# Token-major projections and six gates as seven block products per pair of units, with the last modulation rows made in the merge and the output projection

## The chip, the cores and the metric

The kernel runs on one core of a Trainium2 chip. The metric is device time in microseconds for one execution of the whole layer. Besides the time there is a profile of one execution, with every instruction of each engine: PE (matrix products; PEld are its weight loads), DVE, ACT and POOL (elementwise), and SP, which here issues the DMA transfers.

## The reference

One layer of a backbone over 1024 tokens of width 1024, with 256 context tokens, in float32. What the change touches:

```python
m_lat = (silu(c) @ w_mod + b_mod).reshape(B_, 1, N_MOD, D)     # six modulation rows
h = rms_norm(x, norm_mix) * (1.0 + m_lat[:, :, 1]) + m_lat[:, :, 0]
aq, ak, av, bq, bk, bv, cq, cf, cb, ci, cg, gates = split(h @ w_in)   # gates: 3 branches x 1024
bq, bk = rms_norm(heads(bq), qn), rms_norm(heads(bk), kn)
aq, ak, bq, bk = [apply_rope(t, cos, sin) for t in (aq, ak, bq, bk)]
yc = hgrn2_bidir(cq, cf, cb, ci, cg, ...); ya = window_attn(aq, ak, av, ...); yb = global_attn(bq, bk, bv, ...)
up = einsum('blnw,nwd->blnd', stack([ya, yb, yc]), w_branch)
x_mix = x + m_lat[:, :, 2] * (sum(sigmoid(gates) * up) @ w_out)
h2 = rms_norm(x_mix, norm_ffn) * (1.0 + m_lat[:, :, 4]) + m_lat[:, :, 3]
x = x_mix + m_lat[:, :, 5] * conv_ffn(h2, ...)
```

Modulation rows 0 and 1 are needed ahead of everything; rows 2 to 5 (the kernel's j = 0 to 3) only from the output projection on.

## The kernel before

Every float32 product is made of three products in a shorter format: an operand is split into a high part (a cast on ACT: `wh`, `hh`, `yh`) and the rest (a subtraction on DVE: `wl`, `hl`, `yl`), and PE does high by high, high by low and low by high. `w_unit` loads a weight tile of 128 x 1024 (512 KB, `wr`) and splits it so. `hh` and `hl` hold the whole modulated h: 8 tiles of 128 channels by 1024 tokens.

The stages, in order of time: the modulation rows 0 and 1 and the context to about 100 us; the heads of the recurrence (`hgrn_head`) to 420, and four gate units to 446; then the stage of the change, to about 667; the two attention branches to about 910 and 1200 (`attention`, with the other 14 gate units woven in between its steps as filler); the merge (`merge_up`) to 1325; the output projection (`wo_half`, twice) to 1415; and the gated MLP to the end.

The stage of the change has six token-major units, `tok_major(br)` for br = 0 and 1 with u = 2 (a branch's keys and values) and u = 0, 1 (halves of its queries). A unit takes eight token tiles of 128 tokens, each 24 matmuls (tiles `tm`, 128 x 256: h is the stationary side). Each tile is turned by the rotary table (`rope`: tiles `t`, `qo`) and, for br = 1, first normalized per head (`head_rms`: a square on ACT, a reduction and a scaling on DVE, a power on POOL: tile `hrs`; then the product `qn` on DVE), and stored to `q_d` or `kv_d`. After each unit comes one channel-major gate unit (`gate_unit`, tiles `gz`: 48 matmuls of 128 x 512), evicted by ACT to `gs` and stored to `gate_d`. Woven among these by `weave` is `mod_rest`: for each of four modulation rows eight tiles of `w_mod` (`wmr`) are summed on DVE into `macc`, then PE transposes and DVE reduces them into `mods`.

`merge_up` takes the branches in the order 2, 0, 1. It loads a branch's four tiles of y from `y_d`, splits them into `yh` and `yl`, and does eight units of 24 matmuls (`br`), each multiplied by the sigmoid of a gate tile loaded from `gate_d` (`sgt`) into `xm`. `y_d` is stored by the attention, one token tile (`yT`) at a time. The tiles of y lie in memory that `hh` and `hl` held until the last gate product.

A scheduler places the instructions that the code emits into a fixed order per engine, by its own estimate of when operands are ready and by the priorities in the code (`wprio`). Each engine then takes its instructions strictly in that order. DMA issues are in SP's order.

## Time and profile before

| what | before |
|---|---|
| median of 3 runs | 2082.62 us (2080.54 to 2084.43) |
| profiled execution, its time | 2082.49 us |
| its span | 2080.7 us |
| PE busy | 2038.4 us, 98% |
| DVE busy | 1443.1 us, 69% |
| ACT busy | 1005.1 us, 48% |
| POOL busy | 274.1 us, 13% |
| mean granted PE clock | 0.997 |

The span is what the profile shows from the first to the last instruction; the execution's own time is 1.8 us longer. A row of a timeline gives start, duration, engine, source line, operation, out<-in, and in brackets the idle time of the engine before it with what ended it. Matmul durations overlap, so their rate is read from their starts. A row of a group gives count, busy time, mean nanoseconds, and the engine's idle time before the group's instructions by releaser.

### The profile page before, as it was taken

What the parts mean: (1) busy time and instruction counts of PE and PEld (TensorE: products, weight loads), DVE (VectorE), ACT (ScalarE), POOL (GpSimd) and SP (SyncE); (2) the same over time, 40 slices, a digit from 0 to 9 for tenths busy, and PEclk for the clock granted to TensorE, in tenths of its full rate; (3) what the DMA queues carried; (4) which work ended last, traced back from release to release, by engine and by line L of the source; (5) the groups of instructions that cost most, each with busy time, mean ns of one, the idle gap of its engine ahead of it and who ended that gap; (6) DMA issues with size and microseconds to landing.
All of it is one profiled execution on the core that took longest, in us unless ns stands there. A gap on an engine that the chain in (4) does not pass through costs nothing.

```text
span 2080.7 us, 30085 instructions
## 1 busy us (share of the span) xinstructions
PE 2038.4 (98%) x11501; PEld 1704.3 (82%) x11501; DVE 1443.1 (69%) x2343; ACT 1005.1 (48%) x1742; POOL 274.1 (13%) x247
## 2 busy tenths in 40 slices
PE   8999999999999999999999999999999999999997
PEld 5888888889988888778888788888888888888886
DVE  3836756736566788678888756668767777779964
ACT  3433323311121877688888833445444544444442
POOL 0000000010022122100000000011333344300001
PEclk9999999999999999999999999999999999999999
DMA  9410111136543321211100254552222222268722
GB/s 369 135 48 30 46 51 32 52 107 211 193 146 126 94 62 43 78 64 37 31 31 29 89 189 160 182 169 83 84 85 86 81 81 81 92 221 307 257 75 81
DMA packets 102144, 229.77 MB, mean 110 GB/s; under 512 B 10480, under 2 KB 35440, under 8 KB 100976
## 3 DMA queue, kind: packets, MB, share of 16 engines
q1 hardware_dynamic: 102000, 227.85, 32.9%
q8 instruction: 90, 1.47, 0.3%
q14 instruction: 54, 0.44, 0.1%
HBM read 182.20 MB, written 45.61 MB: 109 GB/s over the span
## 4 chain that ended last, share of the span: by engine, by line
PE 68%; DVE 3%; ACT 2%; issue 1%; DMA 1%; POOL 1%; SPq 0%; DVEq 0%; ACTq 0%; POOLq 0%
PE pp L1460 5%; PE dn L1053 3%; PE dn L1054 3%; PE dn L1052 3%; PE gz L190 3%; PE gz L191 3%; PE gz L192 3%; PE up L909 3%; PE up L911 2%; PE up L910 2%; PE po L1446 2%; PE po L1447 2%; PE br L191 2%; PE br L192 2%; PE br L190 2%; PE upc L911 2%
## 5 line engine op out<-in xcount | busy, mean ns | idle before, releaser
L166 ACT CAST wh<-wr 128x1024 fp32r<-128x1024 f32 x91 | 95.8, 1052 | 282.2 <-PE gz L191 56.3
L167 DVE TENSOR_TENSOR wl<-wr,wh 128x1024 fp32r<-128x1024 f32 x91 | 112.5, 1236 | 105.6 <-ACT wh L166 104.9
L1465 DVE TENSOR_TENSOR pl<-pp,ph 128x512 fp32r<-128x512 f32 x236 | 159.6, 688 | 29.5 <-ACT ph L1464 23.9
L190 PE MATMUL gz<-hh,wh 128*128 128x512 f32 x384 | 156.2, 407 | 3.7 <-ACT gs L580 3.6
L191 PE MATMUL gz<-hl,wh 128*128 128x512 f32 x384 | 152.2, 396 | 0.0
L192 PE MATMUL gz<-hh,wl 128*128 128x512 f32 x384 | 152.1, 396 | 0.0
L1464 ACT CAST ph<-pp 128x512 fp32r<-128x512 f32 x236 | 135.7, 586 | 31.7 <-PE pp L1460 29.0
L1052 PE MATMUL dn<-ac,wh 128*128 128x512 f32 (+2 forms) x311 | 119.3, 384 | 1.3 <-DVE xt L1060 1.2
L1053 PE MATMUL dn<-ac,wh 128*128 128x512 f32 (+2 forms) x311 | 119.3, 383 | 0.5 <-DVE ac L739 0.5
L1054 PE MATMUL dn<-ac,wl 128*128 128x512 f32 (+2 forms) x311 | 119.2, 383 | 0.0
L201 PE MATMUL tm<-wl,hh 128*128 128x256 f32 x384 | 108.9, 284 | 2.0 <-DVE wl L167 2.0
L200 PE MATMUL tm<-wh,hh 128*128 128x256 f32 x384 | 108.7, 283 | 0.0
L202 PE MATMUL tm<-wh,hl 128*128 128x256 f32 x384 | 108.6, 283 | 0.0
L1446 PE MATMUL po<-ph,VHL 128*128 128x512 f32 x236 | 106.1, 450 | 1.5 <-ACT ph L1464 1.1
L1447 PE MATMUL po<-pl,VHL 128*128 128x512 f32 x236 | 97.5, 413 | 0.1
L190 PEld LDWEIGHTS gz<-hh,wh 128*128 128x128 f32 x384 | 72.7, 189 | 17.2 <-ACT gs L580 5.8
L192 PEld LDWEIGHTS gz<-hh,wl 128*128 128x128 f32 x384 | 72.4, 189 | 15.0
L191 PEld LDWEIGHTS gz<-hl,wh 128*128 128x128 f32 x384 | 72.9, 190 | 11.3
L1460 PE MATMUL pp<-ident,plat 128*128 128x128 f32 x512 | 76.7, 273 | 0.0
L1460 PEld LDWEIGHTS pp<-ident,plat 128*128 128x128 f32 x512 | 62.7, 140 | 16.9 <-DVE pl L1465 1.3
L201 PEld LDWEIGHTS tm<-wl,hh 128*128 128x128 f32 x384 | 73.7, 192 | 3.0 <-DVE wl L167 2.7
L190 PE MATMUL br<-yh,wh 128*128 128x512 f32 x192 | 74.3, 390 | 1.4 <-ACT yh L1605 1.4
(1424 smaller groups left out, 5891.2 us busy)
## 6 DMA issues: line engine op xcount, KB each, us to landing
wr<-in_w_cm SPq DMA_DIRECT2D x48, 512.0 KB, 3.8
wr<-in_w_up SPq DMA_DIRECT2D x44, 512.0 KB, 3.5
wmr<-in_w_mod SPq DMA_DIRECT2D x32, 512.0 KB, 4.4
wr<-in_w_dn SPq DMA_DIRECT2D x30, 512.0 KB, 4.7
b<-act_d SPq DMA_DIRECT2D x25, 512.0 KB, 5.7
gate_d<-gs SPq DMA_DIRECT2D x48, 256.0 KB, 2.1
sgt<-gate_d SPq DMA_DIRECT2D x24, 512.0 KB, 3.4
act_d<-u SPq DMA_DIRECT2D x22, 512.0 KB, 2.6
```

The costliest lines, as they stand in the source:

```text
L190: T.matmul(psl, wh[:, k, c], hh[:, k0 + k, cols], start=s, stop=False)
L191: T.matmul(psl, wh[:, k, c], hl[:, k0 + k, cols], start=False, stop=False)
L192: T.matmul(psl, wl[:, k, c], hh[:, k0 + k, cols], start=False, stop=e)
L201: T.matmul(psl, hh[:, k, toks], wl[:, k % 4, :], start=False, stop=False)
L1052: T.matmul(z, w[0][:, c], h[0], start=s, stop=False, **on)
L1053: T.matmul(z, w[0][:, c], h[1], start=False, stop=False, **on)
L1054: T.matmul(z, w[1][:, c], h[0], start=False, stop=e, **on)
L1446: T.matmul(po, vv, ph, start=n == 0, stop=False)
L1447: T.matmul(po, vv, pl, start=False, stop=n == len(kts) - 1)
L1460: T.transpose(pp[:, h], PT(h, n), ident)
L1464: A.copy(ph, pp)
L1465: V.tensor_tensor(out=pl, in0=pp, in1=ph.bitcast(F32), op=ALU.subtract)
```

## The change

The six units and the six gates of the stage become three token-major pairs, `tok_pair`, each followed by a gate pair, `gate_pair`. The token-major pairs are ((0,2),(1,2)), ((0,0),(0,1)) and ((1,0),(1,1)): keys and values of both branches, queries of the windowed branch, queries of the global branch. Two units stacked are one product W h, which is cut into 2 x 2 blocks (a unit and a half of the 1024 channels of h by a half of the tokens) and made of seven block products where eight were before, in the form with shared sums (Winograd's).

The block sums of h are made once: T1 to T4, each with high and low part, by `h_sums`, which is woven with three plain gate units (gates 1 to 3) that stood in the stage ahead before. The sums of weight blocks are made on DVE per pair, ahead of the split (`s`, line 711), four per pair; a pair loads eight weight tiles of half size and makes seven splits (`w_split`, line 634). The products accumulate in two PSUM regions (`tmt..`, `gp`, `gpb`); drains copy (ACT) or add (DVE, lines 762, 836, 838) into tiles `c` in SBUF. The rotary and the norm now run in place on these `c` tiles, as closures kept in a list `behind`; one is taken out after each group of matmuls of later products. Four token tiles are stored by one DMA.

`mod_rest` takes the rows to make and the number of `wmr` buffers. Rows j = 0, 1 are made in `merge_up`, one step per unit, with one buffer; rows j = 2, 3 in `wo_half`, one step per tile, with two buffers. Its transposes come in two groups of four.

```diff
@@ gate_unit
-        def gate_unit(pool, n, i, mode):
+        def gate_unit(pool, n, i, mode, whole=None):
...
+                gs = whole[:, hf] if whole is not None else pool.tile([P, 512], F32, tag="gs", name=f"gs{n}{i}{hf}", bufs=2)
-        def mod_rest(pool):
-
-            for j in range(4):
+        def mod_rest(pool, js, bufs):
+
+            for j in js:
                 acc = pool.tile([P, D], F32, tag="macc", name=f"macc{j}", bufs=1)
                 for k in range(KT):
-                    wm = pool.tile([P, D], F32, tag="wmr", name=f"wmr{j}{k}", bufs=2)
+                    wm = pool.tile([P, D], F32, tag="wmr", name=f"wmr{j}{k}", bufs=bufs)
                     SP.dma_start(wm, ins["w_mod"][k * P:(k + 1) * P, (j + 2) * D:(j + 3) * D])
                     if k == 0:
                         V.tensor_scalar(out=acc, in0=wm, scalar1=scc[:, k, 0:1], scalar2=None, op0=ALU.mult)
                         V.scalar_tensor_tensor(out=acc, in0=wm, scalar=scc[:, k, 0:1], in1=acc,
                                                op0=ALU.mult, op1=ALU.add)
                     yield
-                pm2 = mm2(f"pm2{j}").rearrange("p a (b c) -> p (a b) c", c=P)
-                for i in range(KT):
-                    T.transpose(pm2[:, i], acc[:, i * P:(i + 1) * P], ident)
-                V.reduce_sum(out=mods[:, j], in_=pm2, axis=AX.X)
+                for hf in range(2):
+                    pm2 = bank("a", f"pm2{j}{hf}")
+                    for i in range(4):
+                        T.transpose(pm2[:, i], acc[:, (hf * 4 + i) * P:(hf * 4 + i + 1) * P], ident)
+                    V.reduce_sum(out=mods[:, j, hf * 4:hf * 4 + 4], in_=pm2, axis=AX.X)
                 V.tensor_tensor(out=mods[:, j], in0=mods[:, j], in1=bmod[:, (j + 2) * 8:(j + 3) * 8], op=ALU.add)
-            V.scalar_tensor_tensor(out=af, in0=mods[:, 2], scalar=1.0, in1=gains[:, 1], op0=ALU.add, op1=ALU.mult)
-            yield
+                if j == 2:
+                    V.scalar_tensor_tensor(out=af, in0=mods[:, 2], scalar=1.0, in1=gains[:, 1], op0=ALU.add, op1=ALU.mult)
+                yield
-            for n, i in gates[:4]:
-                for j, _ in enumerate(gate_unit(c1, n, i, "mm")):
-                    if late and j % 8 == 7:
-                        late.pop(0)()
+            for j, _ in enumerate(gate_unit(c1, *gates[0], "mm")):
+                if late and j % 6 == 5:
+                    late.pop(0)()
...
+            hb = {(a, b): [p[:, a * KQ:(a + 1) * KQ, (t1, t2)[b]] for p in H] for a in range(2) for b in range(2)}
+            ht = {n: [hs_.tile([P, KQ, LH], F32R, tag=f"T{n}{p}", name=f"T{n}{p}") for p in "hl"] for n in (4, 3, 2, 1)}
+
+            def ctile(nm):
+                return p3.tile([P, 2, 512], F32, tag="c", name=f"c{nm}", bufs=5)
+
+            def h_sums():
+
+                for k in range(0, KQ, 2):
+                    ks = slice(k, k + 2)
+                    f = {}
+                    for a, b in ((0, 0), (0, 1), (1, 1), (1, 0)):
+                        f[a, b] = ctile(f"h{a}{b}{k}")
+                        V.tensor_tensor(out=f[a, b], in0=hb[a, b][0][:, ks].bitcast(F32),
+                                        in1=hb[a, b][1][:, ks].bitcast(F32), op=add_)
+                        yield
+
+                    def put(n, out, x, y):
+                        V.tensor_tensor(out=out, in0=x, in1=y, op=sub)
+                        split([p[:, ks] for p in ht[n]], out)
+
+                    put(1, f[0, 0], f[0, 1], f[0, 0])
...
+            def plain_gates():
+                for n, i in gates[1:4]:
+                    yield from gate_unit(p3, n, i, "mm", ctile(f"g{n}{i}"))
+
+            weave((plain_gates(), 48), (h_sums(), 16))
+
+            S_ORDER = ((0, 0), 1, 2, (1, 1), 3, (1, 0), 4)
+
+            def pair(nm, W, n, regions, unit, drains, behind):
+
+                def load(t, i, j):
+                    SP.dma_start(t, W(i, j))
+                    return t
+
+                def raw(i, j):
+                    cnt[0] += 1
+                    t = wp.tile([P, 1024], F32, tag="wr", name=f"wr{cnt[0]}", bufs=WR)[:, :KQ * n]
+                    return load(t.rearrange("p (k n) -> p k n", k=KQ), i, j)
+
+                s = p3.tile([P, 1024], F32, tag="s", name=f"s{nm}", bufs=1)[:, :KQ * n].rearrange("p (k n) -> p k n", k=KQ)
+
+                def tt(out, x, y, op=sub):
+                    V.tensor_tensor(out=out, in0=x, in1=y, op=op)
+                    return out
+
+                for q in range(7):
+                    with tc.high_priority(offset=wprio[0] + SPRIO):
+                        if q == 0:
+                            src = raw(0, 0)
+                        elif q == 1:
+                            src = tt(load(s, 1, 0), s, raw(1, 1), add_)
+                        elif q == 2:
+                            src = tt(s, s, raw(0, 0))
+                        elif q == 3:
+                            r = raw(0, 1)
+                            src = tt(r, r, s)
+                        elif q == 4:
+                            src = tt(s, raw(1, 1), s)
+                        else:
+                            src = raw(*((0, 1), (1, 1))[q - 5])
+                        w = w_split(src, KQ, n)
+                    b = S_ORDER[q]
+                    h = hb[b] if isinstance(b, tuple) else ht[b]
+                    for x in range(len(regions(q))):
+                        unit(regions(q)[x], w, h, x, q in (0, 1, 5))
+                        for _ in range(1 if behind else 0):
+                            behind.pop(0)()
+                    drains(q)
...
+            def gate_pair(g0, g1):
+
+                nm = f"{g0[0]}{g0[1]}"
+                idx = [U_C["gate"] + g[0] * 8 + g[1] for g in (g0, g1)]
+                z = mm2(f"gp{nm}")
+                zb = bank("b", f"gpb{nm}", (P, 512))
+                cA, cB = ctile(f"gA{nm}"), ctile(f"gB{nm}")
+                zq = lambda q: zb if q == 5 else z[:, q % 2 if q < 4 else 0]
+
...
+                def drains(q):
+                    z_ = zq(q)
+                    if q in (0, 1, 2, 6):
+                        A.copy({0: cA[:, 0], 1: cB[:, 1], 2: cA[:, 1], 6: cB[:, 0]}[q], z_)
                     else:
+                        c = {3: cA[:, 1], 4: cB[:, 1], 5: cA[:, 0]}[q]
+                        V.tensor_tensor(out=c, in0=z_, in1=c, op=add_)
+                    if q >= 5:
+                        n, i = (g0, g1)[q - 5]
+                        SP.dma_start(gate_d[n, i], (cA, cB)[q - 5].rearrange("p a b -> p (a b)"))
+
+                pair(nm, lambda i, j: ins["w_cm"][idx[i]].rearrange("p (k n) -> p k n", n=P)[:, j * KQ:(j + 1) * KQ], P,
+                     lambda q: [zq(q)] * 2, unit, drains, behind)
...
+            def finish(br, u, hf, c):
+
+                nh = 4 if u < 2 else 2
+
+                def one(t):
+                    nm = f"{br}{u}{hf * 4 + t}"
+                    x = c[:, t, :nh * 64].rearrange("p (h e) -> p h e", h=nh)
+                    if br == 1:
+                        rs = head_rms(nc, p3, c[:, t, :nh * 64], nh, nm, mhalf)
+                        V.tensor_tensor(out=x, in0=x, in1=rs[:, :, None].to_broadcast([P, nh, 64]), op=ALU.mult)
+                    rope(x, nh, hf * 4 + t, None if br == 0 else tabs["q" if u < 2 else "k"], nm)
+
+                def store():
+                    if u == 2:
+                        SP.dma_start(kv_d[br][2 + hf * 4:6 + hf * 4].rearrange("t p n -> p t n"), c)
+                    else:
+                        SP.dma_start(q_d[br][hf * 4:hf * 4 + 4, :, u * 256:(u + 1) * 256].rearrange("t p n -> p t n"), c)
+
+                behind.extend([(lambda t=t: one(t)) for t in range(4)] + [store])
+
+            def tok_pair(a, b):
+
+                nm = f"t{a[0]}{a[1]}"
+                za, zb = (mm2(f"tm{nm}{x}").rearrange("p a (t n) -> p (a t) n", n=256) for x in range(2))
+                zc = [None, None]
+                c = {}
+
...
+                def drains(q):
+                    x = {0: "11", 1: "22", 2: "12", 3: "12", 4: "22", 5: "11", 6: "21"}[q]
+                    if x not in c:
+                        c[x] = ctile(f"{nm}{x}").rearrange("p a (t n) -> p (a t) n", n=256)
+                    if q in (0, 1, 2, 6):
+                        A.copy(c[x], (za, zb)[q % 2])
+                    elif q == 5:
+                        for y in range(2):
+                            V.tensor_tensor(out=c[x][:, 2 * y:2 * y + 2], in0=zc[y], in1=c[x][:, 2 * y:2 * y + 2], op=add_)
+                    else:
+                        V.tensor_tensor(out=c[x], in0=(za, zb)[q % 2], in1=c[x], op=add_)
+                    if q >= 3:
+                        finish(*(a if x[0] == "1" else b), int(x[1]) - 1, c[x])
+
+                pair(nm, lambda i, j: ins["w_tm"][((a, b)[i][0] * 3 + (a, b)[i][1]) * 2 + j].rearrange("p (k n) -> p k n", n=256),
+                     256, regions, unit, drains, behind)
+
+            behind = []
+            for x, (a, b) in enumerate((((0, 2), (1, 2)), ((0, 0), (0, 1)), ((1, 0), (1, 1)))):
+                tok_pair(a, b)
+                gate_pair(*gates[4 + 2 * x:6 + 2 * x])
+            while behind:
+                behind.pop(0)()
...
+            merge_up(nc, mp, ins, gate_d, y_d, xm, half, w_unit, gemm_cm, mm2, mod_rest(mp, (0, 1), 1))
...
                 sumsq(ff, ss, xm[i][:, cols], i, f"m{hf}", 512, 4)
+                next(mr)
+                if i == KT - 1:
+                    next(mr)
...
+        mr = mod_rest(ff, (2, 3), 2)
...
+                next(mr, None)
                 s = mp.tile([P, L], F32, tag="sgt", name=f"sgt{n}{i}")```

Three places show how this moves instructions.

The first is DVE in the work on the queries of the global branch. Before, one token tile after another goes through reduction (L1186), scaling (L1187), product with the norm (L667), rotary (L648, 651, 652):

```order
L1186 TENSOR_REDUCE hrs_5659<-hsq_5657 128x4
L1187 TENSOR_SCALAR hrs_5659<-hrs_5659 128x4
L667 TENSOR_TENSOR qn_5663<-tm_5631,hrs_5659 128x256
L648 TENSOR_TENSOR t_5665<-qn_5663,tbq 128x256 x2
L651 TENSOR_TENSOR qo_5656<-t_5665 128x4x32
L652 TENSOR_TENSOR qo_5656<-t_5665 128x4x32
L1186 TENSOR_REDUCE hrs_5699<-hsq_5697 128x4
```

After, the same operations (L1343, 1344, 792, 778, 780, 781, in place on `ct`) stand among weight sums (L711), weight splits (`wl`, L634) and drains (L836) of the products that run at the time:

```order
L836 TENSOR_TENSOR ct_5039<-tmt10c_5323,ct_5039 128x512
L778 TENSOR_TENSOR t_5404<-ct_5097,tbq 128x256 x2
L634 TENSOR_TENSOR wl_5557<-s_5508,wh_5556 128x512
L780 TENSOR_TENSOR ct_5097<-t_5404 128x4x32
L781 TENSOR_TENSOR ct_5097<-t_5404 128x4x32
L1343 TENSOR_REDUCE hrs_5431<-hsq_5429 128x4
L711 TENSOR_TENSOR s_5508<-s_5508,wr_5586 128x512
L1344 TENSOR_SCALAR hrs_5431<-hrs_5431 128x4
L1343 TENSOR_REDUCE hrs_5468<-hsq_5466 128x4
L792 TENSOR_TENSOR ct_5097<-ct_5097,hrs_5431 128x256
```

A split that a gate product needs (`wl_5557`) now stands behind the rotary of earlier tiles, and the next tile's reduction ahead of this tile's product with the norm.

The second is SP's row where the second attention branch ends. Before, the loads of y stand around the last stores `yT_14` and `yT_15`:

```order
L1483 DMA y_d<-yT_13_11816 128x2x128
L1604 DMA y_12179<-y_d 128x1024
L581 DMA gate_d<-gs_12011 128x512
L1604 DMA y_12185<-y_d 128x1024
L1617 DMA sgt_12232<-gate_d 128x1024
L1617 DMA sgt_12261<-gate_d 128x1024
L1483 DMA y_d<-yT_14_12018 128x2x128
L1604 DMA y_12191<-y_d 128x1024
```

After:

```order
L1640 DMA y_d<-yT_14_11792 128x2x128
L1640 DMA y_d<-yT_15_11916 128x2x128
L1761 DMA y_11953<-y_d 128x1024
L1761 DMA y_11959<-y_d 128x1024
L594 DMA wmr_12007<-in_w_mod 128x1024
L1775 DMA sgt_12010<-gate_d 128x1024
L1761 DMA y_11965<-y_d 128x1024
```

All loads of y now follow the last store, and the modulation weights of the merge stand between them.

The third is PE at the same place (`pp` are transposes of the attention's weights, `po` its products with the values). Before, the merge's first products stand among the last products of the attention:

```order
L1446 MATMUL po_12026<-ph_158_12121,VHL_0_8517 128x512
L190 MATMUL br_12207<-yh_12195,wh_12203 128x512
L191 MATMUL br_12207<-yl_12196,wh_12203 128x512
L192 MATMUL br_12207<-yh_12195,wl_12204 128x512
L1447 MATMUL po_12026<-pl_158_12122,VHL_0_8517 128x512
L1446 MATMUL po_12026<-ph_159_12132,VHL_0_8517 128x512
L190 MATMUL br_12207<-yh_12177,wh_12203 128x512
L1447 MATMUL po_12026<-pl_159_12133,VHL_0_8517 128x512
```

After:

```order
L1603 MATMUL po_11800<-ph_158_11895,VHL_0_8291 128x512
L1604 MATMUL po_11800<-pl_158_11896,VHL_0_8291 128x512
L1603 MATMUL po_11800<-ph_159_11906,VHL_0_8291 128x512
L1604 MATMUL po_11800<-pl_159_11907,VHL_0_8291 128x512
L190 MATMUL br_11981<-yh_11951,wh_11977 128x512
```

No product of the merge stands ahead of the attention's last one.

More of the change, by code (lines that the diff above doesn't have):

```diff
@@ new lines, in build, with split, w_split @@
+        t1, t2 = slice(0, LH), slice(LH, L)
+        def split(parts, src):
+            A.copy(parts[0], src)
+            V.tensor_tensor(out=parts[1], in0=src, in1=parts[0].bitcast(F32), op=ALU.subtract)
+        def w_split(src, nk, ncol):
+            cnt[0] += 1
+            hi, lo = (wp.tile([P, 1024], F32R, tag=t, name=f"{t}{cnt[0]}", bufs=n)[:, :nk * ncol]
+                      .rearrange("p (k n) -> p k n", k=nk) for t, n in (("wh", WH), ("wl", WL)))
+            split((hi, lo), src)
+            return hi, lo
@@ L715, in build @@
             mp = Aligned(sm.enter_context(tc.tile_pool(name="mp", bufs=2, reuse_waits="tile")))
-            merge_up(nc, mp, ins, gate_d, y_d, xm, half, w_unit, gemm_cm, mm2)
+            merge_up(nc, mp, ins, gate_d, y_d, xm, half, w_unit, gemm_cm, mm2, mod_rest(mp, (0, 1), 1))
         pcs = top.enter_context(ExitStack())
@@ L1005, in act @@
             return h
-        def w_split(src, nk, ncol):
-            cnt[0] += 1
-            hi, lo = (wp.tile([P, 1024], F32R, tag=t, name=f"{t}{cnt[0]}", bufs=n)[:, :nk * ncol]
-                      .rearrange("p (k n) -> p k n", k=nk) for t, n in (("wh", WH), ("wl", WL)))
-            split((hi, lo), src)
-            return hi, lo
         def weights(q, u):
@@ L1591, in softmax_global, with merge_up @@
     yield
-def merge_up(nc, mp, ins, gate_d, y_d, mg, half, w_unit, gemm_cm, mm2):
+def merge_up(nc, mp, ins, gate_d, y_d, mg, half, w_unit, gemm_cm, mm2, mr):
     V, A, G, T, SP = nc.vector, nc.scalar, nc.gpsimd, nc.tensor, nc.sync
```

99 lines of the change are left out of this document (51 added, 48 removed).

## The prediction, made before the result was known

> **What bounds the kernel now.** I read the page first, then tables by stretch, the waits of PE, and single rows.
>
> ```profile
> span 2080.7 us, 30085 instructions
> PE 2038.4 (98%) x11501; PEld 1704.3 (82%) x11501; DVE 1443.1 (69%) x2343; ACT 1005.1 (48%) x1742; POOL 274.1 (13%) x247
> 446.30:656.30 210.00, 204.79 (x1444) 191.97 (x1443) 127.87 (x302) 35.26 (x69) 30.72 (x28) 0.99 0.52 167
> 590.06 0.80 PE L190 MATMUL gz<-hh,wh 128*128 128x512 f32 x1 [2.76 <-ACT gs L580]
> 590.00:592.00 2.00, 1.94 (x5) 1.56 (x6) 0.14 (x2) 0.01 (x1) 0.00 (x0) 0.50 0.76 222
> 592.00:594.00 2.00, 2.00 (x8) 1.57 (x7) 0.00 (x0) 0.00 (x0) 0.00 (x0) 0.69 0.57 217
> ```
>
> PE is busy 98% of the span, so products removed shorten it as long as nothing else makes PE wait. The third row is the stage that changes, 446.3 to 656.3 us: busy time of PE, PEld, DVE, ACT and POOL, then granted clock, DMA share and GB/s. PE idles 210.00 - 204.79 = 5.2 us there, 2.76 of it in one wait for an eviction on ACT. After that wait the clock stands at 0.50 and then 0.69 for two stretches of 2 us: 1.0 + 0.6 = 1.6 us more. DVE is busy 127.87 of 210, 61%.
>
> The profiled execution took 2082.49 us, 0.13 below the median of the three runs (2082.62); the sum is made against 2082.49. A difference within 0.2% (4.2 us) I call the same, about what a measurement of this kernel can tell.
>
> **What the change removes from PE.** Each pair of units takes seven half-size block products for eight.
>
> ```profile
> 461.45 0.28 PE L202 MATMUL tm<-wh,hl 128*128 128x256 f32 x1
> 461.57 0.28 PE L200 MATMUL tm<-wh,hh 128*128 128x256 f32 x1
> 461.69 0.28 PE L201 MATMUL tm<-wl,hh 128*128 128x256 f32 x1
> 550.20 0.39 PE L190 MATMUL gz<-hh,wh 128*128 128x512 f32 x1
> 550.43 0.39 PE L191 MATMUL gz<-hl,wh 128*128 128x512 f32 x1
> ...
> 552.02 0.39 PE L192 MATMUL gz<-hh,wl 128*128 128x512 f32 x1
> ```
>
> Starts, not durations, give the rate: 0.12 us for a tm matmul and, from 550.20 to 552.02 in eight steps, 0.227 for a gz matmul. Six token-major units are 6 x 8 x 24 = 1152 matmuls, now 1008: 144 x 0.12 = 17.3 us. Six gates are 288, now 252: 36 x 0.227 = 8.2. Together 25.5 us. The modulation transposes stay 32 and cost the same elsewhere. The old idle and slow clock (5.2 + 1.6) go with the order that made them; what the new order makes is counted below. Credit: 32.3 us.
>
> **What DVE gets.** Its prices, two of its waits, and the end of its last work before the stage:
>
> ```profile
> 427.94 0.75 DVE L1327 SCALAR_TENSOR_TENSOR ys<-oT,gnc,cg 128x512 f32<-128x512 f32 x1 [0.81 <-PE oT L1325]
> DVE qn L667 <- POOL hrs L1188: 21.9, 23, 1.2
> L598 DVE SCALAR_TENSOR_TENSOR macc<-wmr,scc,macc 128x1024 f32<-128x1024 f32 x28 | 35.9, 1281 | 17.4 <-DMA wmr<-in_w_mod 17.2
> L167 DVE TENSOR_TENSOR wl<-wr,wh 128x1024 fp32r<-128x1024 f32 x26 | 31.7, 1220 | 43.0 <-ACT wh L166 43.0
> L166 ACT CAST wh<-wr 128x1024 fp32r<-128x1024 f32 x26 | 27.3, 1052 | 106.8 <-PE gz L191 55.9 <-PE tm L202 22.4 <-issue 20.5
> L1465 DVE TENSOR_TENSOR pl<-pp,ph 128x512 fp32r<-128x512 f32 x13 | 8.8, 683 | 1.2 <-ACT ph L1464 1.1
> 638.23 0.42 DVE L667 TENSOR_TENSOR qn<-tm,hrs 128x256 f32<-128x256 f32 x1 [1.18 <-POOL hrs L1188]
> 641.70 0.42 DVE L667 TENSOR_TENSOR qn<-tm,hrs 128x256 f32<-128x256 f32 x1 [1.19 <-POOL hrs L1188]
> ```
>
> Added: the sums of h, 24 x 1.22 = 29.3 us; weight sums, 4 a pair, 12 x 1.22 + 12 x 0.68 = 22.8; splits, 21 x 1.22 + 21 x 0.68 for 12 + 6 x 1.22 before, +18; accumulating drains, 3 x (2 x 1.22 + 2 x 0.68) + 9 x 0.68 = 17.5. Together 87.6. The modulation rows leave the stage: 28 x 1.28, 4 x 1.0 and their four reductions, -45. So about 127.9 + 43 = 171 us of DVE work stand against some 185 us of PE work: 92% instead of 61%. On average it still fits; a place where DVE's share is above one does not. I followed the new order of each engine by these prices, place by place:
>
> - **Entry.** T1 and T2 need 12 of the 24 h operations and casts between; DVE is free from the end of the last head (428.7 us), and three plain gates, 3 x 10.9 us of PE, cover it. The weight split of the third product stands behind them in DVE's row. Nothing to 3 us; 1.5 taken.
> - **Pair 1** (keys and values of both branches, half of it with the root mean square). In the gate pair PE's row has the first matmuls of the sixth product ahead of the fourth, so it waits for a cast (1.05 at most a wait) and then for the split behind a row of rope operations. 1 to 6; 3.5 taken.
> - **Pair 2** (queries without it): one cast, 0 to 2; 1 taken.
> - **Pair 3** (queries with it) is the dense place. From the end of the fourth token product PE has 144 x 0.12 + 84 x 0.227 = 36 us of work. DVE has 16 row-tiles, two 1024-wide splits, seven 512-wide ones, four sums and drains: 15 us beside the row-tiles. One row-tile took 641.70 - 638.23 = 3.47 us before, 1.2 of it waiting for POOL's power; its own operations are 2.3. The new order puts the reduction of a next tile ahead of the wait of the last, so I take 2.3: 16 x 2.3 + 15 = 52 us, of which three tiles (7 us) stand behind the last split that PE needs. 45 - 36 = 9 us late, spread over several splits, and about 1 of slow clock. At 1.9 a tile (back-to-back starts overlap) it is 3; with a third of the POOL wait left, 16. Taken 10.
> - **Attention lead.** Its key loads now stand on SP behind whole-half stores that wait for the last row-tile. The plain gates of the fill (52 matmuls, 11.8 us) run meanwhile: 0 to 3, 0.5 taken.
>
> **Where the attention ends.** This follows from the order of SP and PE, since y loads now stand behind the last y store. The fourth row below is of the twelve y loads.
>
> ```profile
> 1179.88 0.33 SPq L1604 DMA_DIRECT2D y<-y_d  x1
> 1185.86 0.39 PE L190 MATMUL br<-yh,wh 128*128 128x512 f32 x1
> 1200.02 0.39 PE L1447 MATMUL po<-pl,VHL 128*128 128x512 f32 x1
> 1203.08 0.37 SPq L1483 DMA_DIRECT2D y_d<-yT  x1
> DMA to landing us min/median/max: 3.1/4.2/6.3
> L1605 ACT CAST yh<-y 128x1024 fp32r<-128x1024 f32 x11 | 11.4, 1051 | 8.8 <-DMA y<-y_d 5.6 <-PE br L192 3.2
> L1606 DVE TENSOR_TENSOR yl<-y,yh 128x1024 fp32r<-128x1024 f32 x12 | 14.7, 1222 | 10.8 <-ACT yh L1605 10.7
> ```
>
> Before, the first branch products ran between those of the last attention step, 27 of them up to 1200, on y that SP had loaded from 1179.88 on. In the new order all stand behind it. From the last po: 3.05 us until the store issues (1200.02 to 1203.08, less without the 1.2 us split that stood between: 2), then the load 4.2, the cast 1.05: PE waits 7 to 8 us. Twelve products (2.7 us) later the third y tile, whose buffer waits for the first split, is due another 3 us late. With shorter loads (3.1 is the shortest of twelve) and part of the queue overlapped 5 in all; with both waits whole and the clock low after each 13. Taken 8, the lower part, since the last step also loses its interruptions.
>
> The Trainium skill, "TensorE: Matmul & The Clock Gate", section "HAM oscillation — how this bites in real kernels", warns of PE idle gaps over about 3.4 us, after which TensorE runs at half rate for about as long. By that the gap at the end of attention would cost 1.7 us more, an estimate, and the short ones in pair 3 nothing. The trace here has the clock at 0.50 already after 2.76 us, so the measurement is the stricter.
>
> **Merge and output projection.** A modulation step now follows each merge unit.
>
> ```profile
> 1215.00:1325.00 110.00, 109.92 (x484) 90.49 (x483) 69.48 (x79) 45.03 (x50) 0.00 (x0) 1.00 0.50 164
> wmr<-in_w_mod SPq DMA_DIRECT2D x32, 512.0 KB, 4.4
> ```
>
> A unit is 24 x 0.227 = 5.44 us of PE. DVE goes from 63% to 63% + 1.28 / 5.44 = 87%. One buffer means load and sum in turn: 4.4 + 1.28 + issue = 6 us a step, 0.5 a unit slower than PE over two runs of eight. This lag is behind the units unless PE reaches the transposes of the row before its sum is done: 0 to 4, 1 taken. In the output projection the same steps have two buffers and a sum of 1.28 in 5.44 us; transposes at the half's end may wait: 0 to 4, 0.5 taken.
>
> Sum: 1.5 + 3.5 + 1 + 10 + 0.5 + 8 + 1 + 0.5 = 26.0 lost against 32.3 gained: 6.3 us faster, 2082.49 - 6.3 = 2076.2. With all lower ends the loss is 9 (2059), with all upper ends 51 (2101). They are not likely to fall together.
>
> **Rivals.**
> - *DVE bound by the POOL wait* (slower). If the row-tiles of pair 3 keep their 3.47 us, the 13 tiles ahead of the last needed split take 13 x 1.17 = 15.2 us more: 2091. For it: 23 such waits cost DVE 21.9 us now, hidden only because DVE idles beside PE. Against: the new order has other work between power and use. It ends slower by 0.2% (2086.8) from 0.8 us above my 2.3, at 3.1 us a tile.
> - *The end of attention eats the gain* (the same). Whole waits with low clock, 13 for 8: 2081. For it: nothing on PE's row stands between the last po and the first branch product. Against: loads can land in 3.1.
> - *All is covered* (much faster). If the row-tiles run at 1.9 us (loss 3) and the end costs 5, pair 1 one and the rest nothing, the 32.3 stay but for 9: 2059. For it: DVE idles in the trace for whole microseconds wherever PE is ahead. Against: both chains above are in program order on single queues.
> - *It doesn't save the products.* The order of PE has 1008 for 1152 and 252 for 288; only their rate could differ, and the shapes are the same. No chance of its own.
>
> **Chances.** My forecast with some loss more or less (2063 to 2078) 0.42; all covered 0.08; end of attention or a like sum of terms, within 0.2%, 0.24; POOL wait or other DVE lateness, slower, 0.26. So faster 0.50, same 0.24, slower 0.26. The range runs from between forecast and full cover, 2060, to the DVE rival, 2092; the forecast's own range is 2063 to 2078.
>
> **What the profile after would show.** Token products 1008, 0.12 us apart; DVE above 85% busy between 450 and 640 us; in the third pair PE waiting for DVE splits (L634) some 8 to 10 us in all; a PE gap of 5 to 8 us after the last po, released by the yh cast, and a low clock behind it; no wait above 1 us in merge. Wrong would be: gaps in pair 3 of 20 us (the row-tile), or no gap at the end of attention, or merge units longer than 5.6 us.

## The result and the profile after

The changed kernel took 2103.11 us, the median of 4 runs (2101.23 to 2104.95), beside 2082.07 for the kernel before (4 runs, 2080.54 to 2084.43). The ratio is 1.0100, 95% interval 1.0083 to 1.0117: 21 us slower, where 6.3 us faster was forecast, and outside the range. The profiled execution took 2104.95 us, the longest of the four; its span is 22.5 us longer than the one of before.

The head of the page of the changed kernel, to be laid beside that of before:

```profile
span 2103.2 us, 29756 instructions
PE 2028.2 (96%) x11321; PEld 1684.1 (80%) x11321; DVE 1521.3 (72%) x2440; ACT 1037.1 (49%) x1770; POOL 274.0 (13%) x245
```

PE has 180 matmuls fewer (11501 to 11321), the 144 and 36 of the forecast. Its idle time rose from 42.3 to 75.0 us. Its busy time fell by only 10.2 us where 25.5 of products went: while the clock is low, as in several places below, the same products keep PE busy for longer. Four starts on PE's row divide the 22.5 us of span between the parts of the program:

| start of | before, us | after, us | change up to here | forecast up to here |
|---|---|---|---|---|
| last scores of attention branch 0 (`sa`) | 858.6 | 859.6 | +1.0 | -15.8 |
| first output projection (`wo`) | 1326.6 | 1346.8 | +20.2 | -6.8 |
| first `up` of the MLP | 1417.3 | 1438.3 | +21.0 | -6.3 |
| end of the span | 2080.7 | 2103.2 | +22.5 | -6.3 |

So the stage itself missed by 16.8 us, the end of attention with the merge by 10.2 (+19.2 for +9), and the rest by 1.8.

What PE waited for in the stage, by releaser (total, times, longest; 428 to 700 us):

```profile
PE gp L752 <- ACT cgA L759: 9.9, 4, 4.7
PE gz L190 <- ACT cg L580: 6.9, 2, 6.8
PE gp L752 <- ACT cgB L759: 2.7, 3, 1.0
PE gz L192 <- DVE wl L167: 1.1, 1, 1.1
```

The forecast had named splits on DVE. The trace names evictions on ACT, of plain gates (`cg`) and of gate pairs (`cgA`, `cgB`). The longest of them as single rows of PE's timeline, at the entry, in pairs 1, 2 and 3, and where the attention ends:

```profile
442.73 0.80 PE L190 MATMUL gz<-hh,wh 128*128 128x512 f32 x1 [6.78 <-ACT cg L580]
508.18 0.79 PE L752 MATMUL gp<-T1h,wh 128*128 128x512 f32 x1 [3.58 <-ACT cgA L759]
572.65 0.50 PE L752 MATMUL gp<-T1h,wh 128*128 128x512 f32 x1 [1.01 <-ACT cgA L759]
639.95 0.79 PE L752 MATMUL gp<-T1h,wh 128*128 128x512 f32 x1 [4.68 <-ACT cgA L759]
1204.37 1.22 PE L190 MATMUL br<-yh,wh 128*128 128x512 f32 x2 [8.89 <-ACT yh L1762]
```

After each of the four long gaps the granted clock is low. Stretches of 2 us behind the first, the fourth and the last of these rows (columns as in the prediction's tables by stretch):

```profile
442.00:444.00 2.00, 1.27 (x3) 1.08 (x4) 2.00 (x3) 1.13 (x3) 0.00 (x0) 0.50 0.23 88
444.00:446.00 2.00, 2.00 (x6) 1.54 (x6) 2.00 (x3) 1.26 (x3) 0.00 (x0) 0.50 0.14 53
...
640.00:642.00 2.00, 2.00 (x5) 1.61 (x6) 1.16 (x4) 0.76 (x3) 1.32 (x2) 0.50 0.52 134
642.00:644.00 2.00, 2.00 (x7) 1.51 (x6) 2.00 (x7) 0.60 (x1) 0.80 (x1) 0.50 0.00 1
...
1204.00:1206.00 2.00, 1.59 (x3) 0.88 (x4) 1.60 (x2) 1.76 (x3) 0.00 (x0) 0.50 0.61 248
1206.00:1208.00 2.00, 2.00 (x6) 1.55 (x6) 1.51 (x2) 1.84 (x2) 0.00 (x0) 0.60 0.65 217
```

Busy time by one less the clock gives the loss: at the entry (1.27 + 2.00) x 0.5 and 0.2 more behind it, 1.9 us; in pair 1 1.6, in pair 3 2.1, at the end of attention 1.6. Two more stretches at 0.50, from 658.1 us in pair 3 and from 1303.2 us in the merge, cost 1.7 us each; no gap ahead of them is over 1.2 us (more on them under the clock, below).

**Where the entry's 6.8 us come from.** DVE, POOL and ACT in that stretch:

```profile
433.45 2.31 DVE L666 TENSOR_TENSOR ch<-ch,ch 128x1024 f32<-128x1024 f32 x1
440.10 2.28 DVE L634 TENSOR_TENSOR T1l<-ch,T1h 128x1024 fp32r<-128x1024 f32 x1
442.30 1.21 DVE L666 TENSOR_TENSOR ch<-ch,ch 128x1024 f32<-128x1024 f32 x1
```

```profile
432.46 4.43 POOL L684 TENSOR_TENSOR tbq<-cs,qnb 128x512 f32<-128x512 f32 x2 [5.75 <-DMA cs<-in_rope]
436.85 4.45 POOL L684 TENSOR_TENSOR tbk<-cs,knb 128x512 f32<-128x512 f32 x2
```

```profile
440.21 1.04 ACT L633 CAST T3h<-ch 128x1024 fp32r<-128x1024 f32 x1 [3.37 <-DVE ch L666]
441.16 1.04 ACT L633 CAST wh<-wr 128x1024 fp32r<-128x1024 f32 x1
442.10 0.58 ACT L580 COPY cg<-gz 128x512 f32<-128x512 f32 x1
```

While POOL builds two rotary tables (432.5 to 441.3), a DVE operation of 1024 columns takes 2.3 us instead of 1.2, and one of POOL's 2.2 where in the kernel before it took 1.29 to 1.75 (its four rows for `tbq` and `tbk`). ACT takes its row in order: the eviction for which PE waits (442.10) stands behind a cast that waits for a sum on DVE.

**Where the waits of pairs 1 and 3 come from.** ACT's row at both places:

```profile
506.63 0.51 ACT L1340 ACTIVATE hsq<-ct 128x128 f32<-128x128 f32 x2 [2.66 <-DVE hrs L1343]
507.55 0.57 ACT L759 COPY cgA<-gp 128x512 f32<-128x512 f32 x1
...
639.01 0.42 ACT L1340 ACTIVATE hsq<-ct 128x256 f32<-128x256 f32 x1 [2.24 <-DVE hrs L1343]
639.33 0.57 ACT L759 COPY cgA<-gp 128x512 f32<-128x512 f32 x1
```

The copy stands behind squares of the norm, and these wait until a reduction on DVE frees their buffer. PE's product writes the other half of `gp`, but both halves are one tile (`z = mm2(...)`), and the wait seems to be for the tile as a whole; e2 tests it.

**Where the attention ends.** SP's row:

```profile
1186.14 11.92 SPq L1640 DMA_DIRECT2D y_d<-yT  x2
1198.16 0.91 SPq L1761 DMA_DIRECT2D y<-y_d  x2
1199.12 0.42 SPq L594 DMA_DIRECT2D wmr<-in_w_mod  x1
```

The first row holds both stores, the second of them issued last; then come the loads, as the order of SP said. The reason that the code suggests is a matter of room. The merge's tiles (six `yh`, six `yl`, two `y` and two `sgt` of 4 KB per partition) had filled exactly the 64 KB per partition that `hh` and `hl` leave. `macc` and `wmr` add 8 KB, so the pool reaches into memory that the running attention still uses, and its loads have to come behind. The addresses themselves are in no trace; e3 tests the 8 KB.

### The profile page after: what moved, and what is told of

The parts are those of the page before. It is cut to its first block, busy times and chain, and to the rows that moved or that the text cites. A ratio compares the mean times of both kernels' runs of the same rounds, so it can differ in the third digit from the quotient of the medians.

```text
span 2103.2 us, 29756 instructions
## 1 busy us (share of the span) xinstructions
PE 2028.2 (96%) x11321; PEld 1684.1 (80%) x11321; DVE 1521.3 (72%) x2440; ACT 1037.1 (49%) x1770; POOL 274.0 (13%) x245
## 5 line engine op out<-in xcount | busy, mean ns | idle before, releaser
L167 DVE TENSOR_TENSOR wl<-wr,wh 128x1024 fp32r<-128x1024 f32 x73 | 91.6, 1254 | 84.9 <-ACT wh L166 83.4
L190 PE MATMUL gz<-hh,wh 128*128 128x512 f32 x288 | 117.8, 410 | 8.4 <-ACT cg L580 6.9
L192 PE MATMUL gz<-hh,wl 128*128 128x512 f32 x288 | 114.9, 399 | 1.1 <-DVE wl L167 1.1
L191 PE MATMUL gz<-hl,wh 128*128 128x512 f32 x288 | 114.7, 398 | 0.0
L1603 PE MATMUL po<-ph,VHL 128*128 128x512 f32 x236 | 106.1, 450 | 1.9 <-ACT ph L1621 1.3
L1604 PE MATMUL po<-pl,VHL 128*128 128x512 f32 x236 | 97.9, 415 | 0.3 <-DVE pl L1622 0.2
L190 PE MATMUL br<-yh,wh 128*128 128x512 f32 x192 | 76.3, 399 | 11.2 <-ACT yh L1762 11.0
L191 PE MATMUL br<-yl,wh 128*128 128x512 f32 x192 | 76.5, 399 | 2.0 <-DVE yl L1763 1.9
L633 ACT CAST wh<-wr 128x1024 fp32r<-128x1024 f32 (+1 forms) x42 | 37.6, 897 | 82.2 <-PE tmt L826 22.5
L1617 PE MATMUL pp<-ident,plat 128*128 128x128 f32 x512 | 76.6, 273 | 0.3 <-DVE pl L1622 0.2
L1617 PEld LDWEIGHTS pp<-ident,plat 128*128 128x128 f32 x512 | 62.5, 140 | 17.6 <-DVE pl L1622 2.3
L956 ACT ACTIVATE u<-c,cw 128x1024 f32<-128x1024 f32 x38 | 47.3, 1246 | 58.0 <-DVE c L1111 30.0
L192 PE MATMUL br<-yh,wl 128*128 128x512 f32 x192 | 75.6, 395 | 0.0
L634 DVE TENSOR_TENSOR wl<-wr,wh 128x1024 fp32r<-128x1024 f32 (+1 forms) x42 | 43.1, 1029 | 44.7 <-ACT wh L633 44.7
L190 PEld LDWEIGHTS gz<-hh,wh 128*128 128x128 f32 x288 | 54.9, 191 | 18.0 <-ACT cg L580 7.6
L1209 PEld LDWEIGHTS dn<-ac,wh 128*128 128x128 f32 x311 | 58.4, 188 | 13.1 <-DVE xt L1217 1.0
```

The costliest lines, as they stand in the source:

```text
L167: (lo_eng or V).tensor_tensor(out=lo[:, :n], in0=raw[:, :n], in1=hi[:, :n].bitcast(F32), op=ALU.subtract)
L190: T.matmul(psl, wh[:, k, c], hh[:, k0 + k, cols], start=s, stop=False)
L191: T.matmul(psl, wh[:, k, c], hl[:, k0 + k, cols], start=False, stop=False)
L192: T.matmul(psl, wl[:, k, c], hh[:, k0 + k, cols], start=False, stop=e)
L1209: T.matmul(z, w[0][:, c], h[0], start=s, stop=False, **on)
L1603: T.matmul(po, vv, ph, start=n == 0, stop=False)
```

## The experiments

All times are medians beside runs of the kernel before on the same chip (2081.21 us for e1 to e4, 2081.41 for e5 to e8, 2081.91 for e9 to e12). The three groups ran on three chips, so a difference between e4 and a later run is good to about the 0.7 us by which these medians differ, besides the interval of each.

**e1: the tables built on DVE after the sums, POOL free.**

```diff
+            weave((plain_gates(), 48), (h_sums(), 16))
-                    G.tensor_tensor(out=tb[:, :, :, r], in0=cs, ...)      # ahead of weave
+                    V.tensor_tensor(out=tb[:, :, :, r], in0=cs, ...)      # behind it
```

> The two tables of rotary times norm gain are made by DVE after the sums of h are written, in place of POOL. Theory (shared access): in the changed kernel DVE's 1024-wide operations took 2.3 us for 1.2 only while POOL made these tables (432.5 to 441.3 us), and the late sums held PE for 6.8 us plus 1.9 us of low clock. Then the sums stay at 1.15 to 1.25 us each, that gap shrinks below 1 us, and the time falls by 6 to 9 us, to about 2095 to 2097, although DVE has 2.7 us more to do. Rival (the chain of sums itself is too long for the gates that cover it): the operations stay long or the gap stays above 4 us, and the time falls by 3 us at most.

2102.55 us, ratio 1.0098 (1.0083 to 1.0113). DVE's and PE's rows at the entry:

```profile
433.31 1.22 DVE L666 TENSOR_TENSOR ch<-ch,ch 128x1024 f32<-128x1024 f32 x1
```

```profile
439.37 0.79 PE L190 MATMUL gz<-hh,wh 128*128 128x512 f32 x1 [3.56 <-ACT cg L580]
```

The doubled duration is POOL's doing: without it each of these operations takes 1.22 us. Only half of the gap goes, since the chain of sums itself still holds ACT, and the first `sa` comes 1.7 us earlier (695.6). The time's own change, 0.6 where 6 to 9 were expected, is within the spread of the runs and within what the rival allowed.

**e2: the halves of the gate pair as two tiles.**

```diff
-                z = mm2(f"gp{nm}")
+                z = [bank("a", f"gp{nm}{x}", (P, 512)) for x in range(2)]
```

> The two PSUM regions of a gate pair become two tiles of one bank each, where they were halves of one tile. Theory (false wait): PE waited for the copy of the other region (10 + 2.7 + 0.8 us of waits on drains, with 3.7 us of low clock) because both halves are one tile. Then the waits of gp on ACT cgA and cgB go, the second pair's three waits of 1 us with them, and the time falls by 8 to 14 us. Rival (DVE bound): the products then wait for the weight splits on DVE, which stand behind the rotary and the norm, and the time falls by 4 us at most.

2100.4 us, 1.0088 (1.0073 to 1.0103): 2.7 us less than the changed kernel, where 8 to 14 were expected, and the two intervals overlap. PE's waits in the three pairs (500 to 665 us):

```profile
PE gz L192 <- DVE wl L167: 7.8, 1, 7.8
PE gp L752 <- DVE cgB L762: 4.3, 2, 3.4
PE gp L754 <- DVE wl L634: 4.1, 2, 2.1
PE gp L752 <- ACT cgA L759: 1.3, 1, 1.3
```

The wait for the other half was real (9.9 to 1.3 us), but it had hidden another, as the rival said: DVE is late with splits and drains, and all waits together (18.1 us) are no less than in the changed kernel (16.8). The largest is the plain gate behind pair 3, 7.8 us.

**e3: `macc` and `wmr` in a pool of their own on the other side, so that the merge's pool fits where it was.**

```diff
+            mq = Aligned(sm.enter_context(tc.tile_pool(name="mq", bufs=1, side="right", reuse_waits="tile")))
-            merge_up(..., mod_rest(mp, (0, 1), 1))
+            merge_up(..., mod_rest(mq, (0, 1), 1))
```

> The modulation sum and its buffer in the merge lie in a pool of their own on the other side of the memory; the merge's own pool has its old 64 KB per partition. Theory (the pool outgrew its place): with 8 KB more the pool reached past the memory of hh and hl into tiles of the attention, and the loads of y were placed behind the attention's end. Then y is loaded during the last steps, 27 branch products run among them, the 8.9 us gap and the three short ones behind it (2.2 us) and 2 us of low clock go, and the time falls by 10 to 13 us. Rival (only moved): the loads of the modulation weights on the same queue still hold y or the gate tiles, the gap comes back at another place of the merge, and the time falls by 4 us at most.

2095.09 us, 1.0057 (1.0040 to 1.0074). SP's row again, and what PE waits for from 1170 to 1340 us:

```profile
1181.99 0.33 SPq L1762 DMA_DIRECT2D y<-y_d  x1
...
1189.14 0.37 SPq L1641 DMA_DIRECT2D y_d<-yT  x1
1189.62 3.23 SPq L1762 DMA_DIRECT2D y<-y_d  x2
```

```profile
PE br L191 <- DVE yl L1764: 3.5, 4, 1.8
```

The loads stand between the stores again, no wait for `yh` is left, and from the last `sa` to the first `wo` it takes 475.9 us for 487.2. The 8 KB in that pool were the cause of the wait at the end of attention; 7.8 us beyond the 468.1 of before remain, 3.5 of them waits for `yl` where the merge changes from branch to branch.

**e4: e1, e2 and e3 together.**

> The three edits together. If the three causes are separate, the falls add: 24 to 36 us, to 2067 to 2079, below the 2082 of the kernel before. Rival (one bound behind all three, DVE): the sum falls short of half of what the single edits give together.

2085.71 us, 1.0016 (1.0007 to 1.0025): 17.4 us less than the changed kernel, where the three alone gave 0.6 + 2.7 + 8.0 = 11.3 and 24 to 36 were expected. It is not the rival's one bound behind all three either. By the profiles the last `sa` comes 5.6 us earlier than in the changed kernel, where e1, e2 and e3 alone moved it by -1.4, -1.6 and +0.8: the first two, which act ahead of it, seem to help each other. That DVE's earlier start is worth more once the wait for the other half is gone is the likely reason, not shown apart. What is left in the pairs is the 7.8 us of the gate behind pair 3, 3.5 for `cgB` and 3.1 for splits.

**e5: e4 with the queries of the global branch as second pair, those of the windowed branch as third.**

```diff
-            for x, (a, b) in enumerate((((0, 2), (1, 2)), ((0, 0), (0, 1)), ((1, 0), (1, 1)))):
+            for x, (a, b) in enumerate((((0, 2), (1, 2)), ((1, 0), (1, 1)), ((0, 0), (0, 1)))):
```

> The three edits, and the pair with the norm (queries of the global branch) goes second, the pair of the windowed branch's queries last. Theory (DVE is behind where norm, rotary and gate splits fall together and nothing follows that lets it catch up): with the norm's row-tiles spread over the gate pair and the next token pair, the waits on DVE at the end of the stage (2.1 + 0.6 + 0.4 + 7.8 us with the three edits, and some 3 us of low clock) shrink by more than half, and the time falls by 5 to 10 us below that of the three edits, to 2076 to 2081. Rival (DVE's total over the stage is the bound): as much is waited at other places, in the second gate pair or the third token pair, and the time stays within 3 us.

2082.57 us, 1.0010 (0.9999 to 1.0020), 3.1 less than e4, with overlapping intervals, between what theory and rival expected. The wait of 7.8 is gone; two of 1.25 and 2.81 for splits stand in the token products of the next pair instead. The waits move with the pair that has the norm, and a longer stretch behind it absorbs only a part.

**e6: e4 without the norm of br = 1** (its square, reduction, power and product are left out).

> The three edits, with the norm of the global branch's heads left out (square, reduction, power and the product with it; so queries and keys of that branch are not normalized). It prices the norm where it stands. Theory (DVE behind): the waits of the third pair and of the plain gate behind it, 11 us and 3 us of low clock, go but for 2, and most of the 3.2 us in the first gate pair; the time falls by 11 to 16 us below that of the three edits. Rival (another wait holds the gates there, such as the ring of three weight buffers): it falls by 5 us at most.

2063.99 us, 0.9918 (0.9902 to 0.9935): 21.7 less than e4, where 11 to 16 were expected. The spans of the two profiled executions differ by 24.5, and 22.7 of that is there by the last `sa`. PE's waits in the pairs are then one row:

```profile
PE gp L753 <- DVE cgB L763: 0.4, 1, 0.4
```

Over the whole span DVE has 16.9 us less work (1519.0 to 1502.1 us busy by the pages), and 12.7 us of waiting for POOL's power are gone from its row. On PE's side the 24.5 us are 14.5 of idle time and 6.3 of low clock, and 3.7 more that neither places. The time is more than the norm's own work on DVE: its waits count too, since the square on ACT, the reduction on DVE, the power on POOL and the product on DVE stand in in-order rows with the splits and copies that PE needs behind them. How the 21.7 us divide between work and waits this run doesn't tell, as it takes out both.

**e7: e4 with the modulation weights of the merge in halves of 512 columns, two buffers in the same space.**

```diff
-                    wm = pool.tile([P, D], F32, tag="wmr", name=f"wmr{j}{k}", bufs=bufs)
+                    for x in range(nh):                      # nh = 2 in the merge
+                        wm = pool.tile([P, D // nh], F32, tag="wmr", name=f"wmr{j}{k}{x}", bufs=2)
...
```

> The three edits, and each modulation step of the merge loads and adds two halves of 512 columns in two small buffers, where it had one buffer of 1024. Theory (DVE waits at the head of its row for the one buffer's load, 25 us over the merge, and the splits of y stand behind): DVE's waits for these loads fall under 8 us, the waits of the branch products on yl (2.4 + 0.8 + 0.9 us at the two branch changes) shrink to under 1.5, and the time falls by 2 to 5 us. Rival (the splits are late since DVE has too much work there): the waits on yl stay, and the time stays within 1.5 us or rises by the shorter operations' overhead.

2086.25 us, 1.0023 (1.0012 to 1.0034): no gain. DVE's waits for `wmr` there fell only from 19.9 to 18.0 us, where under 8 were expected. So the halves don't take the waits away, and the run leaves open what these waits cost; e10 tells more.

**e8: e5 and e7 together, with a higher priority for the eviction of the plain gates.**

> The three edits, the heavy pair second, the half steps, and the eviction of the three plain gates given priority over the casts of the sums of h on ACT. If all of it is separate: 2070 to 2078, below the kernel before (2081). If DVE's total is the bound of the stage: 2083 or more.

2083.58 us, 1.0008 (0.9999 to 1.0018): nothing beyond e5. The wait at the entry, at which the priority was aimed, stays at 3.5 us.

**e9: e4 with the norm of two token tiles in one trip to POOL, both trips of a half put into `behind` ahead of its rotary.**

```diff
+                def norms(t):                     # square, two reductions, scaling, one power for tiles t, t + 1
...
-                behind.extend([(lambda t=t: one(t)) for t in range(4)] + [store])
+                if br == 1:
+                    behind.extend([lambda: norms(0), lambda: norms(2)])
+                behind.extend([(lambda t=t: one(t)) for t in range(4)] + [store])
```

> The three edits, and the norm's square, scaling and power are taken for two token tiles at once, both pairs of a half ahead of the products with it: 12 trips to POOL for 24, and none directly ahead of its use. Theory (leaving the norm out gave 21.7 us because DVE stands in its row for the trip to POOL, 12.7 us, and pays the small operations): DVE's waits for hrs fall under 3 us, the waits of the third pair and the plain gate (11 us and the clock) at least halve, and the time falls by 6 to 12 us below that of the three edits, to 2074 to 2080. Rival (the norm's own operations and the place of the splits in DVE's row hold PE, not the trip): DVE waits less for POOL, PE as much for DVE, and the time stays within 3 us.

2080.19 us, 0.9991 (0.9981 to 1.0000), 5.5 less than e4. First the row of what DVE waits for in the pairs, then that of PE:

```profile
DVE ct L805 <- POOL hrs L798: 8.2, 6, 1.8
```

```profile
PE gp L753 <- DVE cgB L763: 8.8, 2, 5.8
```

The waits for POOL fell from 10.8 us in 17 (e4) to 8.2 in 6, not under the 3 that were expected; the 7.8 for the late split went, and a drain is late by 5.8 instead. The edit changes the order of the norm in DVE's row as well as the number of trips, so the 5.5 us are of both.

**e10: e4 with a modulation step only behind units 1 to 6 of a branch in the merge.**

```diff
-                next(mr, None)
+                if 0 < i < 7:
+                    next(mr, None)
```

> The three edits, and the modulation steps of the merge only in the units 1 to 6 of each branch, none in the first and last unit. Theory (the sums stand ahead of the splits of the next branch's y in DVE's row): the waits at the two branch changes (2.4, then 0.5 + 0.8 + 0.9 us) fall under 2 us together and the time by 2 to 3 us. Rival (the splits wait for their load or the cast): no change within 1 us.

2081.48 us, 0.9997 (0.9988 to 1.0006), 4.2 less than e4. PE's waits over the merge, 1200 to 1330 us, are one row; in e4 that row had 4.0 us in three:

```profile
PE br L191 <- DVE yl L1765: 0.2, 1, 0.2
```

The sums of the modulation rows, and their waits for their loads (9.3 us on DVE for 19.9), had stood ahead of the splits of the next branch's y.

**e11: e4 with the order of e5, the norm of e9, the merge of e10 and the priority of e8.**

> The three edits, the norm by two tiles, the heavy pair second, the steps in units 1 to 6, and the plain gates' eviction first on ACT. If these add: 2068 to 2076, below the kernel before (2081). If the sums and splits on DVE bound the stage whatever the norm does: 2079 or more.

2068.88 us (4 runs, 2067.96 to 2069.28), 0.9939 (0.9922 to 0.9955): 13 us faster than the kernel before and 34 than the changed one. Its largest waits from 428 to 1330 us:

```profile
PE tmt L841 <- DVE wl L635: 4.4, 1, 4.4
PE gz L190 <- ACT cg L581: 3.6, 1, 3.6
PE gp L754 <- DVE cgB L764: 3.1, 1, 3.1
```

The last `sa` starts at 840.9 us, 17.7 ahead of before: more than the 15.8 forecast for the change as it stood.

**e12: the kernel before with nothing but the modulation rows moved, in a pool of their own.**

> The kernel before, with the modulation rows alone moved as in the change (rows 0 and 1 in the merge, in a pool of their own beside it; rows 2 and 3 in the output projection); products as before. It tells what the move is worth without the block products. Theory (the merge pays what the old stage gains): the old stage loses its two long waits (2.8 and some 1 us, 1.6 us of clock), the merge gets 4 to 5 us of waits on yl: within 3 us of the kernel before. Rival (the move is a cost of its own, up to the 4.5 us by which the three edits are still slower): 4 us slower or more.

2082.08 us, 1.0004 (0.9994 to 1.0013): no change. The stage gets shorter (last `sa` at 852.4 for 858.6), and the way from there to the first `wo` longer by 9.1 (477.2 for 468.1); the profiled execution, 2087.23, was the longest of its ten. So the move gives no gain by itself: what it frees in the stage it costs behind it, also without the block products.

## Why the prediction was wrong, step by step

| term | forecast, us | measured, us (idle + low clock) |
|---|---|---|
| entry | 1.5 (0 to 3) | 6.8 + 1.9 = 8.7 |
| pair 1 | 3.5 (1 to 6) | 5.0 + 1.6 = 6.6 |
| pair 2 | 1 (0 to 2) | 2.6 |
| pair 3 | 10 (3 to 16) | 9.2 + 2.1 + 1.7 = 13.0 |
| lead of the attention | 0.5 (0 to 3) | 1.0 more than before |
| end of attention | 8 (5 to 13) | 11.1 + 1.6 = 12.7 |
| merge, output projection | 1.5 (0 to 8) | 1.8 + 1.7, and 0.8 of length |

These come to 48.9 us where 26.0 were forecast: every term is above what was taken, and entry, pair 1 and pair 2 are above their upper ends. Over the whole span, net of what the kernel before idled too, PE has 32.7 us more idle time, 8.8 more of low clock (10.6 for 1.8) and 25.5 us less of products. That makes 16.0 us; the span is longer by 22.5, so some 6.5 us are placed by no wait and no clock. Most of them will lie in the stage, where PE starts again after 16 waits up to 700 us; that is not shown apart. The 32 modulation transposes, 0.11 us from start to start, move another 3.5 us out of the stage into the parts behind it, among them the 0.8 of the output projection; the sum is the same, but the stage by itself is worse than its row in the table of starts tells.

- **Products saved: right.** 180 matmuls fewer, at the rate forecast. With the repairs of e4 and the norm out of the way (e6) the last `sa` comes 27.4 us earlier than in the kernel before; with the norm in place the most that a run reached is 17.7 (e11).
- **Entry: the term that failed outright**, 8.7 for 1.5 with 3 as upper end. Two things were left out of its sum: the sums were priced with POOL idle, though POOL's tables stand there in the new order, and ACT's row was not followed, where the evictions stand behind casts that wait for these sums. e1 parts the two: POOL's share of the gap is 3.2 us, the chain of sums has 3.6. Taking POOL's share away moved the time by no more than the spread, so e1 shows where the gap comes from and not what it cost.
- **Pairs 1 to 3: the size nearer, the way to it wrong.** Pairs 1 and 2 are 0.6 us above their upper ends, pair 3 is in its range. For pair 3 "PE waiting for DVE splits (L634) some 8 to 10 us" was to be seen; it was 4.7 us for an ACT copy of a PSUM half that PE's product doesn't touch, and shorter ones. That tile wait was not foreseen and reaches pairs 1 and 2 too. Taken away (e2), it uncovered the lateness of DVE that the forecast spoke of.
- **DVE's utilisation: the added work right, the sign to look for wrong.** From 428 us on DVE has 170.0 us busy (to 665) for 131.0 (to 656.3): 39 us more, where 43 were forecast. But "DVE above 85% busy between 450 and 640 us" didn't come:

```profile
456.00:640.00 184.00, 171.24 (x1210) 158.97 (x1209) 121.21 (x286) 55.25 (x80) 13.38 (x16) 0.98 0.39 124
```

  That is 66%, with PE waiting beside it. DVE was not full, it was late: between 500 and 665 us it waited itself, above all for ACT's casts and POOL's powers:

```profile
DVE wl L634 <- ACT wh L633: 27.9, 11, 4.5
DVE ct L792 <- POOL hrs L1345: 10.7, 18, 1.1
```

  That such waits stood ahead of what PE needed is borne out by e9 and e6 for the norm with its powers; for the casts no run tests it.
- **The slower rival had a part of the mechanism and not its price.** It put 15.2 us on POOL's power alone. DVE waits 12.1 us for it in the changed kernel; half the trips, in another order (e9), gave 5.5, the whole norm (e6) 21.7.
- **End of attention: mechanism right, size at the rival's 13 instead of 8.** Its gap of 8.89 us, released by the `yh` cast, was forecast as 5 to 8. The 0.92, 0.53 and 0.78 behind it and the low clock make up the rest. "Taken 8, the lower part, since the last step also loses its interruptions" was a discount for nothing: the last `po` did come earlier, at 1195 for 1200 us, but the 27 products that had run between stood behind the gap.
- **Merge: 1 was too little.** The forecast looked for the lag at the transposes; PE waited instead for the splits of the next branch's y, which stand behind the sums in DVE's row (e10: without sums at the change of branch 4.2 us of time go, for 1.8 of waits seen in the changed kernel and 4.0 in e4). The sign "no wait above 1 us in merge" failed by one of 1.12.
- **"They are not likely to fall together": wrong.** Losses of 54.8 us (32.3 + 22.5) are above the 51 of all upper ends. The terms of the stage all hang on the same in-order rows of DVE and ACT, so they were no independent draws; that they fell on one side together is what such terms do, and the repairs of e1 and e2 moved the last `sa` further together than one by one.
- **The clock: a term left almost at nothing.** The forecast had allowed 1 us for it in the whole stage; 7.3 were lost there. After gaps of 3.58, 4.68, 6.78 and 8.89 us the clock stood at 0.50, 1.6 to 2.1 us lost each time. The rule of the Trainium skill, "TensorE: Matmul & The Clock Gate", section "HAM oscillation — how this bites in real kernels", fits these four gaps, all above its 3.4 us, and the 1.7 us that the prediction worked out from it for the end of attention stands beside 1.6 measured. It doesn't fit the 2.76 us of the kernel before, nor the two places where short gaps were enough:

```profile
654.65:658.06 3.41, 1.66 (x6) 0.78 (x5) 2.95 (x12) 1.72 (x3) 1.82 (x2) 1.00 0.92 314
658.06:661.48 3.42, 3.42 (x9) 2.64 (x8) 2.85 (x11) 0.00 (x0) 0.94 (x2) 0.50 0.23 81
1299.77:1303.18 3.41, 1.75 (x5) 0.95 (x6) 3.41 (x4) 3.18 (x4) 0.00 (x0) 1.00 0.48 149
1303.18:1306.59 3.41, 3.41 (x9) 2.42 (x9) 3.41 (x4) 0.00 (x0) 0.00 (x0) 0.50 0.22 65
```

  In these traces the clock changes in steps of 3.41 us. The two steps ahead of the low ones had PE idle for 1.75 and 1.66 of the 3.41 us, in gaps of 1.12 us at most. Over all fourteen traces, from 120 to 2060 us, each step at full clock in which PE idled over 55% was followed by a low one, and each under 48% but two (39% both) by a full one. Here the measurement decides: gaps count by their sum in such a step, and short ones that stand close together cost as one long one does.

Left open: the 6.5 us that no row places, the wait at the entry, which stays at 3.5 us or more in every run that has POOL free, and how much of e11's gain over e4 (16.8 us) belongs to each of its four edits.

## What to carry to other kernels

When work moves to an engine with room on average, follow each in-order row to the instruction that the bound engine waits for; 66% busy and 7.8 us late (e2) went together here, and 17 us of work taken out of such a row, with the waits that came with it, returned 22. Halves of a PSUM tile that are used in turn should be two tiles: as one tile they waited for each other, 9.9 us here for 1.3. And before moving a buffer into a pool that reuses memory, compare the pool's size with what it reuses: 8 KB more in that pool put its loads behind a stage that had nothing to do with them, and 8 us came back when they went elsewhere. Short gaps of PE that stand close together are to be added up, because the clock goes down after them too. Terms that hang on the same rows belong in the range as one, not as independent draws.

## What the runs showed of the hardware that was not expected

An elementwise operation of DVE on 128 x 1024 took 2.28 to 2.31 us while POOL worked on its tables, and 1.21 us directly behind them (e1: 1.22 in the same place, with POOL free); POOL's operation of 128 x 512 took 2.2 us in that time, and 1.29 to 1.75 in the kernel before. The two go as if by turns: a turn of 2.28 us is a little less than one of each alone, 1.22 + 1.29 = 2.5. The Trainium skill, "SBUF — State Buffer", section "SBUF: two separate sides", says that the two engines share a port pair as an exclusive lock, held for the whole instruction; these rows agree with it.
